# Layer 0 attention: products with values in groups of five steps instead of four, and two more buffers for exponentials

## The chip, the cores and the metric

The kernel runs on one core of a Trainium2 chip. The metric is the device time of one execution in microseconds (us); lower is better. Matrix products run on TensorE (PE in the profile, its weight loads PEld), elementwise work on VectorE (DVE) and GpSimd (POOL), activations such as the exponential on ScalarE (ACT). SyncE (SP) issues most of the DMA transfers.

## The reference, cut to what matters

Two layers over 2048 latent tokens and 256 context tokens. The even layer (layer 0) runs two branches side by side: latent attention with 8 heads over all 2304 keys, and a gated linear attention ("GLA"), scanned in both directions. The odd layer has a neighbourhood attention. The change is inside the latent attention of layer 0:

```python
s = jnp.einsum('bqhd,bkhd->bhqk', qi, k, preferred_element_type=jnp.float32) * scale
p = jax.nn.softmax(s, axis=-1).astype(v.dtype)
return jnp.einsum('bhqk,bkhd->bqhd', p, v)
```

Scores have 96 components per head, values 64. Context queries see the 256 context keys only; latent queries see all 2304.

## The kernel before, in words

The program is written with a tile framework. It records instructions in the order of the Python code, and a scheduler then puts each engine's instructions into one fixed order, by the program's order, by when it expects data and buffers to be ready, and by explicit "issue after" edges. At run time every engine works through its own list in order and waits on semaphores. So a change in one loop can move instructions of another branch that share its engines.

**Attention of layer 0** (`even_attention`, L867). The 8 heads are taken as 4 pairs, `j` = 0 to 3. Each pair has five query blocks, `nb` = 0 to 4: one of 256 context tokens (two key tiles) and four of 512 latent tokens (18 key tiles each). One key tile of one block is a **step**; a pair has 2 + 4 x 18 = 74 steps, the whole attention 296. A step does, for each of the two heads `i`:

- three matmuls into one of three PSUM buffers `st` (L980 to L982): high part of keys by high part of queries, high by low, low by high. Keys are the stationary operand, so scores come out transposed, keys on partitions;
- one exponential on ACT into a buffer `apt` of 128x512 (L984, shown at L106, the line of the helper);
- one addition on DVE into `acc`, the running sum of exponentials (L971).

The products with values come later. Each step is put on a list `pend` (L989). When `pend` holds six steps, the oldest four go through `tail` (L916): for each step and head one product (L922) of values (64 columns, stationary) with the exponentials, accumulated in PSUM `av`. Head 0 fills rows 0 to 63 of the PSUM tile, head 1 rows 64 to 127. In the trace every such product is two records of MATMUL, so a group of four steps, 8 products, shows as `x16`. Two steps after the last tail of a block, `end` (L927) runs `finish` (L849): a product `den` (L854) for the row sums, a reciprocal through Ln and Exp on ACT, three DVE operations (L859 to L861), one multiplication on POOL (L863) and the store.

**Loads.** `queries` (L907) loads one block of queries into one of two buffers `aq`: 96 rows of four parts (L910) and one further row (L911), both issued by SP. A block's load can start when the scores of the block two before it are done. At a new pair, the block of 512 queries after the context block therefore waits for the last scores of the previous pair, and so does the last third of the keys' low part (`akl`, L892), which SP issues ahead of it. The context block in between has two steps only. Values come as `av<-Vn` (L899) in thirds.

**What else runs.** The GLA (`gla`, L686) shares all engines. Per chunk of 128 tokens PE runs L722 and L728 (gates), L739 and L743 (cumulative sums), L766 (transposes), L776 (scores inside the chunk), L785 and L791 (products with values), with ACT and DVE steps between them. After the last chunk DVE walks the backward scan (L814 to L816: three operations for each of 16 chunks); only when it is done does the output loop go on (L830: product with the scanned state, L842: transposes), because its output tile takes a buffer of the scan. `even_mix` (L1009) also splits the output weights in this time (`wraw<-w_out`, L380 and L383), and after the attention it runs the projection.

Of the kernel before, what the change touches and what calls it, by code (L numbers as in the profile page):

```python
# [17 lines left out]
P = 128  # L18
# [70 lines left out]
class Kern:  # L89
# [777 lines left out]
    def even_attention(self, ap, pp):  # L867
        nc = self.nc
        blocks = [(0, CTX, [0, 1])] + [(CTX + 512 * b, 512, list(range(NT))) for b in range(4)]
        TT = NT // 3  # L870
        W = TT * P
        ring = [self.tl(ap, [P, 2, W], f"akh{n}", F32R, bufs=1) for n in range(4)]
        self.att_free = ring[0]
        for kh in ring:
            nc.gpsimd.memset(kh[A_QK : A_QK + 1].bitcast(F32), 1.0)
        K, L, V = {}, {}, {}

        def parts(j, p):
            return ((0, W // 2), (W // 2, W)) if j + p == 0 else ((0, W),)

        def keys(j, p):

            K[j, p] = kh = ring[(3 * j + p) % 4]
            for a, b in parts(j, p):
                nc.sync.dma_start(kh[:A_QK, :, a:b].bitcast(F32),
                                  self.KT[2 * j : 2 * j + 2, 0, :A_QK, p * W + a : p * W + b].rearrange("h p t -> p h t"))
                yield

        def low(j, p):
            L[j, p] = kl = self.tl(ap, [P, 2, W], "akl", F32R, bufs=3)  # L890
            for a, b in parts(j, p):
                nc.sync.dma_start(kl[:A_QK, :, a:b].bitcast(F32),  # L892
                                  self.KT[2 * j : 2 * j + 2, 1, :A_QK, p * W + a : p * W + b].rearrange("h p t -> p h t"))
                yield

        def values(j, p):
            V[j, p] = v = self.tl(ap, [P, TT, P], "av", bufs=4)
            for a, b in parts(j, p):
                nc.sync.dma_start(v[:, a // P : b // P, :], self.Vn[:, (p * W + a) // P : (p * W + b) // P, j * P : j * P + P])  # L899
                yield  # L900

        def load(*gens):
            for g in gens:
                for _ in g:
                    pass

        def queries(j, q0, w):  # L907

            q = self.tl(ap, [P, 4, 512], "aq", F32R, bufs=2)
            nc.sync.dma_start(q[:A_QK, :, :w].bitcast(F32), self.QT[2 * j : 2 * j + 2, :, :A_QK, q0 : q0 + w].rearrange("h z p t -> p (h z) t"))  # L910
            return q, nc.sync.dma_start(q[A_QK : A_QK + 1, 0::2, :w].bitcast(F32),  # L911
                                        self.QT[2 * j : 2 * j + 2, 0, A_QK : A_QK + 1, q0 : q0 + w].rearrange("h p t -> p h t"))

        pend, late, O = [], [], {}

        def tail(j, nb, n, kt, pts):  # L916

            w, kts = blocks[nb][1:]
            if n == 0:
                O[j, nb] = self.tl(pp, [P, 512], "av", bufs=2)  # L920
            for i in range(2):
                nc.tensor.matmul(O[j, nb][i * 64 : i * 64 + 64, :w], V[j, kt // TT][:, kt % TT, i * 64 : i * 64 + 64], pts[i][:, :w],  # L922
                                 start=n == 0, stop=n == len(kts) - 1)
            if n == len(kts) - 1:
                late.append([2 if nb else 5, j, nb])

        def end(j, nb):  # L927
            q0, w, _ = blocks[nb]
            zt = self.tl(ap, [P, 512], "azt", bufs=2)
            nc.sync.dma_start(zt[:, :w], self.zaT[j, :, q0 : q0 + w])  # L930
            self.finish(O.pop((j, nb))[:, :w], sums.pop((j, nb)), zt[:, :w], self.RT[j, :, q0 : q0 + w], w, ap, pp, ("den", 1))

        def step_late():
            for x in late:
                x[0] -= 1
                if x[0] <= 0:
                    end(*x[1:])
            late[:] = [x for x in late if x[0] > 0]

        early, sums, first = {}, {}, {}  # L940
        for j in range(4):
            if j == 0:
                early[0], _ = queries(0, 0, CTX)
                gens = [keys(0, 0), low(0, 0), values(0, 0)]
                for g in gens:
                    next(g)
                early[1], _ = queries(0, CTX, 512)
                for g in gens:
                    next(g)
                for p in (1, 2):  # L950
                    load(keys(0, p), low(0, p), values(0, p))
            else:
                load(low(j, 2), values(j, 1), values(j, 2))
            for nb, (q0, w, kts) in enumerate(blocks):
                if j == 0 and nb in early:
                    Q = early.pop(nb)
                else:
                    Q, last = queries(j, q0, w)
                if j < 3 and nb in (2, 3):
                    with self.tc.issue_after(last.ins):  # L960
                        load(keys(j + 1, 0) if nb == 2 else values(j + 1, 0))
                yield
                acc = [self.tl(ap, [P, 512], f"acc{i}") if nb else self.tl(ap, [P, CTX], f"accc{i}", bufs=1) for i in range(2)]

                def add(n, pts):
                    for i in range(2):
                        if n == 0:
                            first[i] = pts[i]
                        else:
                            a = first[i] if n == 1 else acc[i]  # L970
                            nc.vector.tensor_tensor(out=acc[i][:, :w], in0=a[:, :w], in1=pts[i][:, :w], op=ALU.add)  # L971

                for n, kt in enumerate(kts):
                    pts = []
                    kq = slice(kt % TT * P, kt % TT * P + P)
                    kh, kl = K[j, kt // TT], L[j, kt // TT]
                    for i in range(2):
                        qh, ql = Q[:, 2 * i, :], Q[:, 2 * i + 1, :]
                        ps = self.tl(pp, [P, 512], "st", bufs=3)
                        nc.tensor.matmul(ps[:, :w], kh[: A_QK + 1, i, kq], qh[: A_QK + 1, :w], start=True, stop=False)  # L980
                        nc.tensor.matmul(ps[:, :w], kh[:A_QK, i, kq], ql[:A_QK, :w], start=False, stop=False)  # L981
                        mm = nc.tensor.matmul(ps[:, :w], kl[:A_QK, i, kq], qh[:A_QK, :w], start=False, stop=True)  # L982
                        pt = self.tl(ap, [P, 512], "apt", bufs=14)
                        self.act(pt[:, :w], ps[:, :w], AF.Exp, scale=A_SCALE)  # L984
                        pts.append(pt)
                    add(n, pts)
                    if n == len(kts) - 1:
                        sums[j, nb] = [a[:, :w] for a in acc]
                    pend.append((j, nb, n, kt, pts))  # L989
                    with self.tc.issue_after(mm.ins):  # L990
                        step_late()
                        if len(pend) == 6:
                            for _ in range(4):
                                tail(*pend.pop(0))
                    if nb == 4 and j < 3 and n % TT == TT - 1 and n < NT - 1:
                        load(keys(j + 1, n // TT + 1), low(j + 1, n // TT))
        yield mm
        while pend:
            tail(*pend.pop(0))
        while late:  # L1000
            step_late()
# [759 lines left out]
```

## Time and profile before

| what | value |
|---|---|
| median of 3 runs | 3673.76 us (3667.17 to 3674.72) |
| the profiled execution | 3676.2 us |
| its span | 3674.1 us |
| mean granted clock of TensorE | 0.982 |
| attention of layer 0 on PE | from 1086.0 to about 1982 us of the span |

The span is the stretch of the profiled execution that the profiler covers; 2.1 us of that execution lie outside it. In the views, a row of the order of time gives start, duration, engine, line, operation, output and inputs, and in brackets how long the engine sat idle before it and who released it. Matmuls are pipelined: each record lasts longer than the distance to the next, so distances between starts are what PE spends.

### The profile page before, as it was taken

How to read it: one execution, taken by the hardware profiler on the slowest of the kernel's cores; microseconds unless marked ns; L12 is line 12 of the kernel's file. 1: busy time of each engine (PE TensorE's matmuls, PEld its weight loads, DVE VectorE, ACT ScalarE, POOL GpSimd, SP SyncE). 2: the span in 40 equal slices, each digit the busy share in tenths (PEclk: the TensorE clock that was granted, in tenths of full speed). 3: DMA queues.
4: the chain of work that ended last, by engine and by line, in shares of the span. 5: the costliest groups of instructions: out<-in, count | busy, mean ns of one | idle time of the engine just before them, and what ended most of it. 6: DMA issues, size and time to landing. Idle time of an engine off the chain costs nothing.

```text
span 3674.1 us, 51831 instructions
## 1 busy us (share of the span) xinstructions
PE 3565.7 (97%) x18404; PEld 2758.7 (75%) x18404; DVE 2363.0 (64%) x4860; ACT 1437.0 (39%) x2741; POOL 1205.6 (33%) x1336
## 2 busy tenths in 40 slices
PE   8999999999999999999999999999899999999998
PEld 6988998888886666655556878888688887555577
DVE  4677666888876666687664444454578784666721
ACT  5545551111125555555553124444422223555510
POOL 1433330101111212122201233333334443777743
PEclk9999999999999999999999999999999999999899
DMA  7455472222241232243622544455744447788554
GB/s 253 145 155 155 133 210 87 80 73 88 75 137 53 83 98 79 85 115 109 177 67 96 188 161 123 141 157 160 227 146 122 146 120 190 210 215 219 175 178 149
DMA packets 364372, 512.19 MB, mean 139 GB/s; under 512 B 25825, under 2 KB 243889, under 8 KB 358210
## 3 DMA queue, kind: packets, MB, share of 16 engines
q1 hardware_dynamic: 322642, 425.49, 39.8%
q0 software_dynamic: 19872, 55.92, 5.1%
q10 hardware_dynamic: 21600, 27.46, 2.1%
q8 instruction: 146, 2.39, 0.3%
q14 instruction: 112, 0.92, 0.1%
HBM read 329.38 MB, written 179.37 MB: 138 GB/s over the span
## 4 chain that ended last, share of the span: by engine, by line
PE 69%; issue 15%; POOL 5%; DVE 5%; DMA 4%; ACT 2%; SPq 0%; POOLq 0%; DVEq 0%; ACTq 0%
PE av L922 7%; PE gm L129 6%; PE gm L130 6%; PE gm L131 6%; PE st L980 4%; PE st L981 4%; PE st L982 4%; PE st L129 2%; PE st L131 2%; PE st L130 2%; PE pj L131 2%; PE pj L130 2%; PE pj L129 2%; PE o L1456 2%; DMA wraw<-w_od 1%
## 5 line engine op out<-in xcount | busy, mean ns | idle before, releaser
L971 DVE TENSOR_TENSOR acc<-acc,apt 128x512 f32<-128x512 f32 x512 | 364.8, 737 | 153.5 <-ACT apt L106 150.6
L106 ACT ACTIVATE apt<-st 128x512 f32<-128x512 f32 (+1 forms) x592 | 344.6, 594 | 290.5 <-PE st L982 257.4
L662 DVE TENSOR_REDUCE mm<-mx 128x1 f32<-128x512 f32 (+1 forms) x656 | 393.2, 630 | 89.9 <-PE mx L661 81.8
L922 PE MATMUL av<-apt,av 128*64 128x512 f32 (+1 forms) x1184 | 286.4, 599 | 0.0
L980 PE MATMUL st<-aq,akh 97*128 97x512 f32 (+1 forms) x592 | 255.7, 432 | 9.7 <-DMA aq<-QT 6.1
L661 PE MATMUL mx<-mk,mq 96*128 96x512 f32 (+1 forms) x656 | 238.6, 372 | 0.0
L981 PE MATMUL st<-aq,akh 96*128 96x512 f32 (+1 forms) x592 | 236.7, 400 | 0.0
L982 PE MATMUL st<-aq,akl 96*128 96x512 f32 (+1 forms) x592 | 235.3, 398 | 0.0
L1330 DVE CUSTOM_DVE_ANT_1 mx<-mx,mtab 128x217 f32<-128x217 f32 (+11 forms) x576 | 184.6, 338 | 49.2 <-PE mx L1324 37.9
L106 ACT ACTIVATE opt<-opt 128x930 f32<-128x930 f32 (+9 forms) x144 | 119.2, 830 | 248.0 <-POOL opt L1627 141.0
L106 ACT ACTIVATE u<-gm 128x352 f32<-128x352 f32 (+1 forms) x144 | 70.5, 496 | 360.4 <-PE gm L131 208.7
L1587 DVE TENSOR_TENSOR opt<-st,tab 128x64 f32<-128x64 f32 (+10 forms) x576 | 142.8, 316 | 88.2 <-PE st L1424 58.1
L922 PEld LDWEIGHTS av<-apt,av 128*64 128x64 f32 x1184 | 81.9, 138 | 156.4 <-issue 154.8
L980 PEld LDWEIGHTS st<-aq,akh 97*128 97x128 f32 x592 | 113.5, 192 | 101.6 <-issue 49.5
L1462 POOL TENSOR_TENSOR oacc<-oacc,opt 128x682 f32<-128x682 f32 (+10 forms) x144 | 169.8, 1199 | 26.4 <-ACT opt L106 25.1
L982 PEld LDWEIGHTS st<-aq,akl 96*128 96x128 f32 x592 | 114.6, 194 | 25.8
L661 PEld LDWEIGHTS mx<-mk,mq 96*128 96x128 f32 x656 | 122.7, 188 | 11.7
L981 PEld LDWEIGHTS st<-aq,akh 96*128 96x128 f32 x592 | 115.3, 195 | 18.3
L1423 PE MATMUL st<-q,kt 128*128 128x480 f32 (+5 forms) x256 | 99.6, 391 | 23.8 <-DVE opt L1587 18.9
L106 ACT ACTIVATE x<-px,modB,modA 128x128 f32<-128x128 f32 x272 | 99.3, 469 | 58.1 <-PE px L331 46.3
L129 PE MATMUL gm<-w0h,hhi 128*128 128x512 f32 x288 | 116.1, 403 | 0.0
L129 PE MATMUL gm<-w1h,hhi 128*128 128x512 f32 x288 | 115.7, 402 | 0.0
(570 smaller groups left out, 9928.1 us busy)
## 6 DMA issues: line engine op xcount, KB each, us to landing
q<-Q SPq DMA_DIRECT2D x48, 512.0 KB
H<-x ACTq DMA_DIRECT2D x36, 512.0 KB
adaw<-ada_w SPq DMA_DIRECT2D x64, 256.0 KB
x<-H SPq DMA_DIRECT2D x32, 512.0 KB
wraw<-w_od SPq DMA_DIRECT2D x64, 256.0 KB
K1t<-okt POOLq DMA_DIRECT2D x32, 512.0 KB, 7.6
kt<-K1t SPq DMA_DIRECT2D x32, 512.0 KB
mtab<-rpb_q SPq DMA_DIRECT2D x16, 899.0 KB
```

Source lines behind the costliest of these rows:

```text
L106: return self.nc.scalar.activation(out, in_, func, **kw)
L129: self.nc.tensor.matmul(out, lh(k), rh(k), start=j == 0, stop=False)
L130: self.nc.tensor.matmul(out, lh(k), rl(k), start=False, stop=False)
L131: yield self.nc.tensor.matmul(out, ll(k), rh(k), start=False, stop=j == n - 1)
L661: mm = nc.tensor.matmul(ps[:, :w], q[:A_QK, (t % 6) * P : (t % 6) * P + P], k[:A_QK, k0 : k0 + w], start=True, stop=True)
L662: nc.vector.tensor_reduce(out=m[:, t, n : n + 1], in_=ps[:, :w], axis=AX.X, op=ALU.max)
L922: nc.tensor.matmul(O[j, nb][i * 64 : i * 64 + 64, :w], V[j, kt // TT][:, kt % TT, i * 64 : i * 64 + 64], pts[i][:, :w], start=n == 0, stop ...
L971: nc.vector.tensor_tensor(out=acc[i][:, :w], in0=a[:, :w], in1=pts[i][:, :w], op=ALU.add)
L980: nc.tensor.matmul(ps[:, :w], kh[: A_QK + 1, i, kq], qh[: A_QK + 1, :w], start=True, stop=False)
L981: nc.tensor.matmul(ps[:, :w], kh[:A_QK, i, kq], ql[:A_QK, :w], start=False, stop=False)
L982: mm = nc.tensor.matmul(ps[:, :w], kl[:A_QK, i, kq], qh[:A_QK, :w], start=False, stop=True)
L1330: nc.vector.tensor_tensor_reduce(out=s, in0=s, in1=tb[:, ri : ri + rn, ci : ci + cn], scale=1.0, scalar=-3e38, op0=ALU.add, op1=ALU.max, a ...
```

## The change

The list of pending steps is allowed to grow to seven, and five steps then go through `tail` in one group. Two buffers are added for the exponentials, since two more of them are held. Nothing is computed differently: each of the 592 products (L922) is still there.

```diff
-                        pt = self.tl(ap, [P, 512], "apt", bufs=14)
+                        pt = self.tl(ap, [P, 512], "apt", bufs=16)
...
-                        if len(pend) == 6:
-                            for _ in range(4):
+                        if len(pend) == 7:
+                            for _ in range(5):
                                 tail(*pend.pop(0))
```

A full group is 10 products in place of 8. With six as the limit, groups go out at steps 6, 10, 14 and so on, counted over all pairs; with seven at steps 7, 12, 17 and so on.

## The prediction

> **What bounds the kernel now.** I read the page first, for the busy shares and the groups of the attention, then the busy time by stretch.
>
> ```profile
> span 3674.1 us, 51831 instructions
> PE 3565.7 (97%) x18404; PEld 2758.7 (75%) x18404; DVE 2363.0 (64%) x4860; ACT 1437.0 (39%) x2741; POOL 1205.6 (33%) x1336
> ...
> L971 DVE TENSOR_TENSOR acc<-acc,apt 128x512 f32<-128x512 f32 x512 | 364.8, 737 | 153.5 <-ACT apt L106 150.6
> ...
> L922 PE MATMUL av<-apt,av 128*64 128x512 f32 (+1 forms) x1184 | 286.4, 599 | 0.0
> ```
>
> ```profile
> core 0: us, PE busy (x) PEld busy (x) DVE busy (x) ACT busy (x) POOL busy (x), PEclk, DMA share, GB/s
> 1096.00:1585.00 489.00, 487.56 (x2520) 308.78 (x2519) 328.52 (x464) 269.42 (x540) 101.31 (x98) 1.00 0.30 87
> 1585.00:1675.00 90.00, 84.73 (x362) 49.42 (x361) 86.12 (x124) 43.72 (x79) 13.53 (x10) 0.96 0.27 76
> 1675.00:1982.00 307.00, 302.16 (x1364) 183.62 (x1365) 195.38 (x291) 167.50 (x332) 58.44 (x57) 0.97 0.38 107
> ```
>
> The attention has three stretches. In the first, 489 us, PE is busy 487.56 us and DVE two thirds: PE bounds it. In the second, 90 us, DVE walks the scan of the GLA and is busy 86.12 us: there DVE bounds, and PE time saved is not gained. In the third PE bounds again. So the change can gain only PE time in the first and third stretch, and can lose where PE waits.
>
> **What a group costs.** In the order of time on PE:
>
> ```profile
> 1704.83 0.40 PE L982 MATMUL st<-aq,akl 96*128 96x512 f32 x1
> 1705.15 3.65 PE L922 MATMUL av<-apt,av 128*64 128x512 f32 x16
> 1708.74 0.50 PE L980 MATMUL st<-aq,akh 97*128 97x512 f32 x1
> 1709.08 0.39 PE L981 MATMUL st<-aq,akh 96*128 96x512 f32 x1
> 1709.31 0.40 PE L982 MATMUL st<-aq,akl 96*128 96x512 f32 x1
> ...
> 1734.19 0.40 PE L982 MATMUL st<-aq,akl 96*128 96x512 f32 x1
> 1734.51 1.08 PE L854 MATMUL den<-acc,mtwos 128*64 128x512 f32 x4
> 1735.52 0.50 PE L980 MATMUL st<-aq,akh 97*128 97x512 f32 x1
> 1735.86 0.40 PE L981 MATMUL st<-aq,akh 96*128 96x512 f32 x1
> ```
>
> Score matmuls start 0.23 us apart (1709.08 to 1709.31). From the L982 ahead of a group to the L981 behind it 4.25 us pass; without a group it would be 0.46, so 8 products cost 3.79. A `den`, two products of the same shape, costs 1.67 less 0.46, 1.21. Eight products are four pairs, two are one: three pairs cost 2.58, one pair 0.86, and what is left, **0.35 us, is the fixed price of a run**. A larger group saves that price.
>
> A group that the scheduler cuts at an odd product loses more: seven products take 3.58 us, as eight do, and the eighth alone 1.00.
>
> ```profile
> 1311.89 3.65 PE L922 MATMUL av<-apt,av 128*64 128x512 f32 x14
> 1315.47 0.66 PE L766 MATMUL gl<-ident,gkt 128*128 128x128 f32 x4
> ...
> 1316.17 1.07 PE L922 MATMUL av<-apt,av 128*64 128x512 f32 x2
> 1317.17 0.39 PE L980 MATMUL st<-aq,akh 97*128 97x256 f32 x1
> ```
>
> I count in the instruction order of the built kernels. Before: 90 runs of L922 that take the time of 311 pairs (the 592 products are 296 pairs; cuts waste 15). After: 72 runs, 307 pairs. In PE time that is 18 x 0.35 + 4 x 0.86 = 9.7 us. Of it two runs and two pairs (2.4 us) lie in the scan stretch; a `den` (1.2 us) also leaves that stretch for the first. What counts is 9.7 - 2.4 - 1.2 = **6.1 us**. Five steps' worth of single scores (3.5 us) move from the third stretch into the first, which is neutral. In the scan stretch DVE's list between the second and last scan step is 117 operations in place of 121: three of 256 columns (0.43) and one of 512 (0.69) fewer, **2.0 us**.
>
> ```profile
> 1602.13 0.69 DVE L971 TENSOR_TENSOR acc<-acc,apt 128x512 f32<-128x512 f32 x1
> 1602.73 0.43 DVE L859 TENSOR_TENSOR den<-den,rc 128x256 f32<-128x256 f32 x1
> ```
>
> The two buffers keep the slack: at a group's start 14 tiles of 16 are held, where 12 of 14 were. They add no instruction, so I put them at zero. They shift the later tiles by 4 KB, and the projection's tiles then lie over other old ones; an estimate from the 0.69 us of one DVE operation bounds what a few later releases cost by 0 to 2 us. The stretch of the scan also ends in a wait of PE and a half clock of 10.24 us (rows further down); DVE's scan sets that moment before and after, and I leave it, with half of a 6.8 us step of the clock, 3.4 us, as its bound to either side.
>
> **What a group hid.** At a new pair of heads the block of 512 queries waits for a buffer that the last scores of the old pair free, and its load is issued only then, behind `akl`:
>
> ```profile
> 1558.08 0.40 PE L982 MATMUL st<-aq,akl 96*128 96x512 f32 x1
> 1560.08 3.65 PE L922 MATMUL av<-apt,av 128*64 128x512 f32 x16
> 1566.95 0.47 PE L980 MATMUL st<-aq,akh 97*128 97x512 f32 x1 [1.24 <-DMA aq<-QT]
> ...
> 1782.14 0.77 PE L980 MATMUL st<-aq,akh 97*128 97x512 f32 x1 [4.84 <-DMA aq<-QT]
> ```
>
> ```profile
> 1312.37 0.44 SPq L910 DMA_DIRECT2D aq<-QT  x1
> ```
>
> ```profile
> 1558.88 7.98 DMA aq<-QT
> ...
> 1771.16 10.89 DMA aq<-QT
> ```
>
> From issue to use the load takes 7.98 us at pair 2 and 10.89 at pair 3. At pair 1 it was issued at 1312.37 and its user started at 1320.49 without a wait: at most 8.1. Before, a group stood in each of the three gaps: groups go out at steps 74, 150 and 222, and pairs begin after 74, 148 and 222. After, they go out at 72 and 77, at 147 and 152, and at 222: **pairs 1 and 2 lose their cover of 3.6 us, pair 3 gets 0.86 us more.** In the new order the gap holds, besides 12 scores of the context block (0.12 each, 1.44), at pair 1 L791, L739, L743 and L766 twice four, at pair 2 L776, L728 and L785:
>
> ```profile
> 1569.29 0.87 PE gl L739 x4
> 1570.15 0.79 PE gl L743 x8
> ...
> 1574.36 0.88 PE gl L766 x8
> ...
> 1578.55 1.09 PE gl L776 x16
> ...
> 1583.81 0.89 PE gl L785 x8
> 1584.70 0.91 PE gl L791 x8
> ```
>
> With 0.4 for changes of shape (an estimate) that is 5.3 us at pair 1 and, with 0.24 for L728, 4.0 at pair 2, against a landing 8.4 us after the release (0.4 to the issue, 7.98). PE then idles 3.1 us at pair 1, none before, and 4.4 at pair 2, 1.2 before: **+3.1 and +3.2 us**. Bounds: the GLA's own waits can't make it more, since they lie inside; a load landing at 5.3 makes it 0 and -1; one of 10.9 adds 2.9 to each. Pair 3: **-0.9**. Behind the waiting L980 all of PE's list is queued, and ACT behind it.
>
> **The clock.** PE's granted clock falls behind such waits:
>
> ```profile
> 1564.95:1568.37 3.42, 2.18 (x13) 1.81 (x13) 1.39 (x2) 1.58 (x3) 1.72 (x1) 1.00 1.07 238
> ...
> 1595.67:1599.09 3.42, 1.87 (x9) 1.07 (x8) 3.29 (x5) 2.04 (x5) 2.17 (x2) 1.00 0.17 61
> 1599.09:1605.91 6.82, 6.82 (x18) 3.65 (x19) 6.70 (x11) 3.43 (x7) 1.61 (x1) 0.50 0.29 77
> ...
> 1674.18:1684.42 10.24, 9.62 (x27) 5.76 (x29) 5.96 (x10) 5.89 (x15) 2.92 (x3) 0.50 0.27 78
> ```
>
> A stretch of 3.42 us with 2.18 busy kept the full clock; one with 1.87 was followed by 6.82 us at half. So a wait above about 1.5 us in such a stretch costs half of 6.8, 3.4 us. Pair 2's wait should bring this in full, **+3.4**; pair 1's, split by GLA work, half of it, **+1.7** (bounds 0 and 5.1, half of the 10.24).
>
> [...]
>
> **The sum.** -6.1 - 2.0 + 3.1 + 3.2 - 0.9 + 3.4 + 1.7 = **+2.4 us**. Against the profiled execution (3676.2, its span 3674.1 and 2.1 outside) that is 3678.6; the median, 3673.76, lies 2.4 us lower and gives 3676.2. I say 3677, no measurable change: about 0.2%, 7.3 us, is what a measurement of this kernel can tell.
>
> **The rivals.**
>
> - *The loads land in time* (faster). If the query loads of pairs 1 and 2 land within 5.3 and 4.0 us of the release, no new wait arises and pair 2's old one goes: -6.1 - 2.0 - 0.9 - 1.2 = -10.2, 3664. For it: nothing shows when pair 1's load landed. Against: 7.98 and 10.89. Chance 0.10.
> - *The waits come, the clock stays.* Without 3.4 and 1.7 the sum is -2.7, 3671. For it: both waits are cut up by GLA work, and the stretch with 2.18 busy. Against: the one with 1.87. [...] Chance 0.17, nearly all within 0.2%.
> - *The loads land late* (slower). In the new order the last thirds of values (L899), freed by later tails, are issued just ahead of pair 2's queries, and a chunk of the GLA's input just behind pair 1's. If both loads then take pair 3's 10.89 us, each wait grows by 2.9 and pair 1's clock falls in full, +1.7: +2.4 + 5.8 + 1.7 = +9.9, 3684 on the median, 3686 on the profiled execution; it decides from about 9.6 us on (2.4 + 1.7 + twice 1.6 passes 7.3). For it: the same load took 7.98 and 10.89 by what ran beside it. Against: at pair 3 the load of a gate row (L1120) went out just before, which the other two gaps don't have. Chance 0.20.
> - *Longer groups starve DVE in the scan stretch.* A group lasts 0.9 us longer, without new exponentials; if DVE runs dry six times, +5.2, and 3682. Against: DVE was busy 86.12 of 90 us there across groups of 3.6. Chance 0.08.
> - That the scheduler undoes the grouping is settled by the built order: 44 of 72 runs have all ten products.
>
> The forecast keeps 0.45. **Range**: from 3664 (loads in time) to 3689 (late loads, 3686, and the scan stretch's bound of 3.4). **Chances**: faster 0.17 (0.10 and the forecast's lower edge), slower 0.28 (0.20, half of the starving, and the upper edge), same 0.55.
>
> **What would show it.** In the profile after: L922 as `x20` in the third stretch, 4.65 us in all (five pairs of 0.86 and 0.35); no group between the last scores of pairs 0 and 1 and the next pair's first block of 512; L980 there with idle time ended by `aq<-QT`, of about 3 and 4 us, and a half clock behind; pair 3's wait down to about 4. Wrong it would be if those waits are absent or above 6 us, if the clock falls elsewhere in the first stretch, or if the scan stretch lengthens.

## The result, and the profile after

The changed kernel took 3681.78 us (median; 3675.30 to 3687.67) beside 3673.03 us of the kernel before: ratio 1.0029, 95% interval 1.0022 to 1.0037. Measured once more: 3679.88 beside 3671.46 us, 1.0019 (1.0009 to 1.0030). So it is slower by some 8.6 us, a quarter of a per cent. The forecast was +2.4 us and "no measurable change"; the time lies inside its range, on the slow side, but both intervals leave out 1: the change can be measured, and that was not forecast.

The page of the changed kernel (group rows: count, busy us, mean ns of one, then the idle time before them):

```profile
span 3679.9 us, 51810 instructions
...
L922 PE MATMUL av<-apt,av 128*64 128x512 f32 (+1 forms) x1184 | 276.5, 594 | 0.0
L980 PE MATMUL st<-aq,akh 97*128 97x512 f32 (+1 forms) x592 | 254.4, 430 | 12.7 <-DMA aq<-QT 10.2
```

The same 1184 records of L922 take 9.9 us less than before (286.4); in the mean of three profiles of either order of PE, 285.4 and 276.9, it is 8.5. The change does what it says. The second row holds the other side: PE's idle time ahead of L980, most of it ended by the query load.

Busy time by stretch, cut near the same events as in the prediction's table (the columns are the same):

```profile
core 0: us, PE busy (x) PEld busy (x) DVE busy (x) ACT busy (x) POOL busy (x), PEclk, DMA share, GB/s
1096.00:1599.00 503.00, 494.99 (x2558) 317.28 (x2558) 333.19 (x474) 272.93 (x549) 101.82 (x100) 0.99 0.30 85
1599.00:1683.00 84.00, 76.64 (x337) 45.67 (x337) 81.46 (x117) 41.57 (x75) 11.48 (x9) 0.98 0.27 74
1683.00:1985.00 302.00, 294.73 (x1346) 180.16 (x1346) 205.10 (x288) 164.17 (x327) 61.76 (x57) 0.98 0.39 108
```

The first stretch is 14 us longer (489 before), the scan stretch 6 shorter (90), the third 5 shorter (307). Cut exactly at the first and third group of L830, the three differences are +12.6, -3.9 and -5.1. The first stretch also holds more work: 2558 matmul records for 2520. In the first, 1.44 us of 489 were idle on PE; now 8.01 of 503 are.

The three gaps at new pairs, in the order of time on PE (start, duration, instruction; in brackets the idle time before it and what ended it). At pair 1 no group of L922 stands between the last scores of the old pair and the first block of 512:

```profile
1308.49 0.40 PE L982 MATMUL st<-aq,akl 96*128 96x512 f32 x1
...
1311.92 0.95 PE L743 MATMUL gl<-ind,gG 128*128 128x2 f32 x8
1313.52 0.63 PE L766 MATMUL gl<-ident,gqt 128*128 128x128 f32 x4 [0.65 <-DVE gqt L753]
1314.97 1.09 PE L766 MATMUL gl<-ident,gkt 128*128 128x128 f32 x4 [0.82 <-DVE gkt L753]
1317.29 0.77 PE L980 MATMUL st<-aq,akh 97*128 97x512 f32 x1 [1.24 <-DMA aq<-QT]
...
1318.28 0.63 PE L982 MATMUL st<-aq,akl 96*128 96x512 f32 x1
1318.71 0.63 PE L980 MATMUL st<-aq,akh 97*128 97x512 f32 x1
```

PE idles 0.65 + 0.82 + 1.24 = 2.71 us, where it did not idle before. The first two pieces name the GLA, but they lie within the time in which the load is on its way. Behind the wait scores start 0.43 us apart (1318.28 to 1318.71) and not 0.23: the half clock, granted from 1314.87 on (rows below). Pairs 2 and 3:

```profile
1558.54 0.40 PE L982 MATMUL st<-aq,akl 96*128 96x512 f32 x1
...
1562.88 1.13 PE L785 MATMUL gl<-gu,gat 128*128 128x128 f32 x8 [0.99 <-PE gl L728]
1567.07 0.47 PE L980 MATMUL st<-aq,akh 97*128 97x512 f32 x1 [3.07 <-DMA aq<-QT]
...
1767.73 4.51 PE L922 MATMUL av<-apt,av 128*64 128x512 f32 x20
...
1781.11 0.77 PE L980 MATMUL st<-aq,akh 97*128 97x512 f32 x1 [5.90 <-DMA aq<-QT]
```

4.06 us of idle time at pair 2 (1.24 before). At pair 3 the group is there, `x20`, and yet PE idles 5.90 us, more than the 4.84 of before. The loads behind these waits, from the chains of waits of the three gaps (start, us):

```profile
1309.29 7.90 DMA aq<-QT
...
1559.35 7.63 DMA aq<-QT
...
1769.28 11.69 DMA aq<-QT
```

Each gap brings a stretch at half clock (granted clock 0.50): from 1314.87, 1567.45 and 1779.08 on, at pairs 1 and 3 before the wait is over, which ends at 1317.29 and 1781.11. The rows of 3.41 us ahead of them are at full clock (stretch, its length, PE busy; PEclk and DMA share are the third and second numbers from the end):

```profile
1311.46:1314.87 3.41, 2.04 (x18) 1.74 (x16) 2.84 (x3) 2.45 (x8) 3.24 (x3) 1.00 1.06 247
1314.87:1321.70 6.83, 5.50 (x14) 3.07 (x16) 1.47 (x2) 1.79 (x3) 1.38 (x3) 0.50 1.06 254
1564.04:1567.45 3.41, 0.38 (x2) 0.36 (x3) 0.57 (x1) 0.60 (x1) 0.00 (x0) 1.00 1.07 248
1567.45:1570.86 3.41, 3.41 (x10) 2.65 (x9) 0.00 (x0) 1.19 (x2) 0.00 (x0) 0.50 1.06 252
1775.67:1779.08 3.41, 0.00 (x0) 0.00 (x0) 1.44 (x3) 0.57 (x2) 1.20 (x2) 1.00 1.15 218
1779.08:1785.91 6.83, 4.80 (x11) 3.80 (x12) 0.00 (x0) 1.72 (x3) 0.00 (x0) 0.50 0.96 268
```

The load isn't late by itself, the 16 DMA engines are busy while it is under way: their share is 0.96 to 1.15 in these rows, at 218 to 268 GB/s.

### The profile page after: what moved, and what is told of

Its sections match the earlier page's. It is cut to its first block, busy times and chain, and to the rows that moved or that the text cites. A ratio compares the mean times of both kernels' runs of the same rounds, so it can differ in the third digit from the quotient of the medians.

```text
span 3679.9 us, 51810 instructions
## 1 busy us (share of the span) xinstructions
PE 3561.2 (97%) x18404; PEld 2761.6 (75%) x18404; DVE 2373.2 (64%) x4860; ACT 1436.8 (39%) x2741; POOL 1208.2 (33%) x1336
## 4 chain that ended last, share of the span: by engine, by line
PE 68%; issue 14%; DVE 6%; DMA 5%; POOL 3%; ACT 3%; SPq 0%; POOLq 0%; DVEq 0%; ACTq 0%
PE av L922 7%; PE gm L129 6%; PE gm L130 6%; PE gm L131 6%; PE st L980 4%; PE st L981 3%; PE st L982 3%; PE o L1456 2%; PE st L129 2%; PE st L131 2%; PE st L130 2%; PE st L1423 2%; PE pj L129 2%; PE pj L131 2%; PE pj L130 2%
## 5 line engine op out<-in xcount | busy, mean ns | idle before, releaser
L971 DVE TENSOR_TENSOR acc<-acc,apt 128x512 f32<-128x512 f32 x512 | 378.0, 766 | 126.3 <-ACT apt L106 123.6
L922 PE MATMUL av<-apt,av 128*64 128x512 f32 (+1 forms) x1184 | 276.5, 594 | 0.0
L980 PE MATMUL st<-aq,akh 97*128 97x512 f32 (+1 forms) x592 | 254.4, 430 | 12.7 <-DMA aq<-QT 10.2
L982 PE MATMUL st<-aq,akl 96*128 96x512 f32 (+1 forms) x592 | 236.0, 399 | 0.0
L1330 DVE CUSTOM_DVE_ANT_1 mx<-mx,mtab 128x217 f32<-128x217 f32 (+10 forms) x576 | 184.3, 338 | 46.4 <-PE mx L1324 37.8
L922 PEld LDWEIGHTS av<-apt,av 128*64 128x64 f32 x1184 | 81.9, 137 | 157.1 <-issue 154.9
L980 PEld LDWEIGHTS st<-aq,akh 97*128 97x128 f32 x592 | 113.8, 192 | 85.8 <-issue 44.1
L982 PEld LDWEIGHTS st<-aq,akl 96*128 96x128 f32 x592 | 114.7, 194 | 25.6
L981 PEld LDWEIGHTS st<-aq,akh 96*128 96x128 f32 x592 | 115.3, 195 | 18.8
```

Source lines behind the costliest of these rows:

```text
L1330: nc.vector.tensor_tensor_reduce(out=s, in0=s, in1=tb[:, ri : ri + rn, ci : ci + cn], scale=1.0, scalar=-3e38, op0=ALU.add, op1=ALU.max, a ...
```

## The experiments

**Theory A**: in the gaps of pairs 1 to 3, PE waits for the query load, because groups of five go out beside the gaps and not in them, and behind each wait the half clock doubles the loss. **Theory B**: the two buffers, by shifting later tiles, delay the work behind the attention. **Theory D**: the loss lies elsewhere. C, that the load's time doesn't depend on what is ahead of it in the queue, is the rival on the repair; in the expectations of the first four runs C still stands for the prediction's rival that longer groups starve DVE. Where an expectation names a wait of an earlier profile, its figure can be up to 1.0 us above the idle time of the rows.

All ratios are against the kernel before. "Attention" runs from the start of the first score to that of the last L922. "Half clock" is the sum of such stretches inside it, without the one of 3.4 to 10.2 us that in 11 of the 14 profiles begins within 2.1 us of the first score. "Behind" is the rest of the span. All three come from one profile each, of a run that can lie 10 us off its median (that of `e4_shift` took 3683.50).

| kernel | median us, ratio (95%) | attention | half clock | behind |
|---|---|---|---|---|
| before; its second profile | see above | 885.7; 887.1 | 23.9; 20.5 | 1702.4; 1698.1 |
| changed; measured again | 1.0029 (1.0022 to 1.0037); 1.0019 (1.0009 to 1.0030) | 889.4; 892.7 | 23.9; 27.3 | 1705.4; 1705.9 |
| e1_buffers | 3672.65, 1.0002 (0.9994 to 1.0011) | 882.9 | 17.1 | 1699.6 |
| e2_five14 | 3681.76, 1.0027 (1.0017 to 1.0036) | 891.0 | 30.7 | 1701.4 |
| e3_cover | 3666.61, 0.9982 (0.9973 to 0.9991) | 879.2 | 10.2 | 1699.4 |
| e4_shift | 3673.86, 1.0008 (0.9998 to 1.0017) | 886.0 | 17.1 | 1707.7 |
| e5_aqfirst4 | 3668.19, 0.9986 (0.9975 to 0.9996) | 882.3 | 23.9 | 1697.4 |
| e6_aqfirst5 | 3671.40, 0.9993 (0.9985 to 1.0002) | 879.1 | 20.5 | 1703.8 |
| e7_both | 3663.10, 0.9972 (0.9961 to 0.9984) | 871.6 | 6.8 | 1702.2 |
| e8_values | 3678.10, 1.0015 (1.0005 to 1.0024) | 887.2 | 23.9 | 1704.5 |
| e9_akl | 3671.48, 1.0000 (0.9991 to 1.0009) | 875.5 | 17.1 | 1703.5 |
| e10_fill | 3679.94, 1.0019 (1.0010 to 1.0029) | 891.7 | 23.9 | 1701.4 |

### The two parts of the change, each alone

`e1_buffers`: the kernel before with 16 buffers.

```diff
-                        pt = self.tl(ap, [P, 512], "apt", bufs=14)
+                        pt = self.tl(ap, [P, 512], "apt", bufs=16)
```

> Groups of four as before, sixteen buffers for the exponentials: the second half of the change alone. Theory A (uncovered query loads): no group moves, so the time of before within 0.1%, about 3673 us, and no wait at pairs 1 and 2 beyond the 1.2 us of before. Theory B (the shift of later tiles by 4 KB costs something in the projection and the odd layer): slower than before by 3 to 8 us, all of it behind 1972 us of the span. Theory C (longer groups starve DVE and ACT): 3673 us, as A.

`e2_five14`: the changed kernel with 14 buffers.

```diff
-                        pt = self.tl(ap, [P, 512], "apt", bufs=16)
+                        pt = self.tl(ap, [P, 512], "apt", bufs=14)
```

> Groups of five with the fourteen buffers of before: the first half of the change alone. Theory A: the waits at pairs 1 and 2 stay as in the changed kernel (3.5 and 4.5 us), the time too, 3680 to 3682 us; at a full list every buffer is held, which may add 1 to 3 us where ACT waits for a buffer. Theory B: the later tiles lie as before, so 3674 to 3677 us. Theory C: as the changed kernel or slower.

The buffers alone change nothing (1.0002), and the groups alone lose the whole (1.0027). Theory B falls; the buffers are worth zero, as the prediction had it.

### The cover alone, and its loss without groups of five

`e3_cover`: the changed kernel, with a first group of two steps, so that groups of five go out at steps 74, 149 and 224 and again cover all three gaps.

```diff
-        pend, late, O = [], [], {}
+        pend, late, O, size = [], [], {}, [4]
...
-                        if len(pend) == 7:
-                            for _ in range(5):
+                        if len(pend) == size[0]:
+                            size[0] = 7
+                            while len(pend) > 2:
```

> The changed kernel with a first group of two steps once four are pending, then groups of five: groups go out at steps 74, 149 and 224 and stand again in all three gaps between pairs. Theory A: waits at pair 1 gone, at pair 2 under 1.5 us, at pair 3 at most 6; the clock no longer falls at pairs 1 and 2; 8 to 11 us less than the changed kernel, 3671 to 3674 us, so as before or a little faster. Theory B: 3680 us still, the loss being behind the attention. Theory C: 3680 us still.

3666.6 us: about 15 less than the changed kernel and 6 less than before. Pair 2's gap, in the order of time on PE:

```profile
1555.29 0.40 PE L982 MATMUL st<-aq,akl 96*128 96x512 f32 x1
...
1556.32 4.51 PE L922 MATMUL av<-apt,av 128*64 128x512 f32 x18
...
1561.18 1.07 PE L922 MATMUL av<-apt,av 128*64 128x512 f32 x2
1563.89 0.40 PE L980 MATMUL st<-aq,akh 97*128 97x512 f32 x1
```

The first score of the new block comes 8.6 us after the last of the old pair, as late as without a group (8.53), but without idle time and without a half clock behind it (the scores there start 0.23 to 0.24 us apart). What the load needs is the same; the group fills it. At pair 3 a wait of 4.14 us remains, and at pair 1 one of 1.77, which theory A had gone: there SP issued the last third of values (L899, 1312.75) between `akl` (1311.73) and the query load (1313.17), and the first score came 11.2 us after the last of the old pair (8.8 in the changed kernel, 8.9 in the one before). Of the 16.4 us between the spans of the changed kernel and of this one, 10.2 lie in the attention and 6.0 behind it, where the order of PE's instructions in the odd layer is again that of before; so not all of the gain is the cover's.

`e4_shift`: groups of four as before, shifted by a first group of three steps, so that they go out at 73, 77, 149, 221 and 225 and leave gaps 1 and 3 uncovered.

```diff
-        pend, late, O = [], [], {}
+        pend, late, O, size = [], [], {}, [5]
...
-                        if len(pend) == 6:
-                            for _ in range(4):
+                        if len(pend) == size[0]:
+                            size[0] = 6
+                            while len(pend) > 2:
```

> Groups of four and fourteen buffers as before, but with a first group of three steps, so that groups go out at steps 73, 77, 149, 221 and 225: pairs 1 and 3 lose their cover, pair 2 keeps it. Theory A: a new wait of 2 to 4 us at pair 1 with a half clock behind it, the wait at pair 3 up from 4.8 to about 8 us, pair 2 as before; 6 to 9 us slower than before, 3679 to 3682 us. Theory B and C: the size of the groups and the buffers are those of before, so 3673 us.

The waits came where theory A put them (pairs 1 and 3, none at pair 2):

```profile
1320.74 0.47 PE L980 MATMUL st<-aq,akh 97*128 97x512 f32 x1 [3.44 <-DMA aq<-QT]
...
1779.01 0.77 PE L980 MATMUL st<-aq,akh 97*128 97x512 f32 x1 [7.94 <-DMA aq<-QT]
```

The time did not follow: 1.0008, as theories B and C had it. PE idles 18.8 us in its attention, 11.7 to 13.7 in three profiles with the order of before, but in its order the scheduler cuts fewer groups at odd places. Its L922 runs number 84 and take the time of 303 pairs (90 and 311 before): at the prediction's prices 6 x 0.35 + 8 x 0.86 = 9.0 us less, about what was expected as the loss; the records of L922 are busy 278.8 us, 6.6 less than the mean of before. That this paid for the waits is argued and not shown. So the run shows the waits and not their price: that a shift changes where groups are cut was left out of its expectation.

### What is ahead of the query load

`e5_aqfirst4` (the kernel before) and `e6_aqfirst5` (the changed kernel) both issue `akl` and the later thirds of values behind the first 512-query load of a new pair. Their scores stand two lines lower, at L982 to L984.

```diff
-                load(low(j, 2), values(j, 1), values(j, 2))
+                pass
...
                     Q, last = queries(j, q0, w)
+                    if j and nb == 1:
+                        load(low(j, 2), values(j, 1), values(j, 2))
```

> Groups of four as before; only the load order at a new pair changes: the last third of the keys' low part (akl, 96 x 2 x 768 values, 590 KB) and the two later thirds of values are issued behind the first 512-query load of the pair and not ahead of it. Theory A (PE waits at new pairs for this query load, and the 590 KB ahead of it in the queue are a good part of its 8 to 11 us): the load lands about 3 us earlier, the wait of 1.5 us at pair 2 goes, that of 5.1 us at pair 3 shrinks to about 2, and half a step of half clock goes with them: 3 to 8 us less than before, 3665 to 3670. Theory C (the load's time is its own latency or the traffic of the other queues, not what is ahead of it): the waits stay and the time is that of before, ratio 1.000.

> Groups of five, 16 buffers, and the query load of a new pair ahead of akl as in the run with groups of four. Theory A (what the change loses, it loses in waits for this load at pairs 1, 2 and 3: about 3.7, 4.7 and 6.2 us in its profile, and in the half clock behind them): each shrinks by about 3 us and most of the half clock goes, 8 to 13 us less than the changed kernel, 3668 to 3674, at or below the kernel before. Theory D (the loss lies elsewhere, in the scan stretch or behind the attention): the time stays within 3 us of the changed kernel's 3682.

The times came as theory A had them: 3668.2 and 3671.4, the latter 8.5 us below the changed kernel of the same measurement. The same edit gains 3.3 us in the kernel before and 8.5 in the changed one, so 5.2 of the 8.4 us between these two hang on this load. The half clock did not go: 23.9 and 20.5 us are left. The two loads of the changed order, from the chains of waits of `e6_aqfirst5`, took 7.90 and 7.63 us before the edit:

```profile
1311.57 5.96 DMA aq<-QT
...
1556.91 5.52 DMA aq<-QT
```

About 2 us less, some 2.4 us earlier counted from the release, since the issue of `akl` is no longer ahead: an estimate from the 590 KB and the 248 to 254 GB/s of the rows at pairs 1 and 2 is 2.3 to 2.4 us. Theory C falls.

`e9_akl` moves `akl` alone, `e8_values` the values alone.

```diff
-                load(low(j, 2), values(j, 1), values(j, 2))
+                load(values(j, 1), values(j, 2))
...
+                    if j and nb == 1:
+                        load(low(j, 2))
```

> The changed kernel with akl alone behind the first 512-query load of a new pair; the values stay ahead. Theory A (the 590 KB of akl ahead of the query load make the waits): nearly all of the 8.5 us that both loads together gained, 3671 to 3674; from the last scores of the old pair to the first of the new block about 6.5, 6 and 10 us in place of 9.2, 9.0 and 13.6. Rival (the values made half of it): 3676 to 3678.

3671.5: moving `akl` alone in the program gives the whole repair. From the last score of the old pair to the first of the new block 6.2, 6.5 and 7.6 us pass, where the changed kernel had 8.8, 8.5 and 13.7. The third figure, expected at 10, is not `akl`'s alone: in the built order the last third of values went behind the query load of pair 3 as well (L910 at 1761.55, L899 at 1763.66).

```diff
-                load(low(j, 2), values(j, 1), values(j, 2))
+                load(low(j, 2))
...
+                    if j and nb == 1:
+                        load(values(j, 1), values(j, 2))
```

> The changed kernel with the loads of the two later thirds of values behind the first 512-query load of a new pair; akl stays ahead of it. In the built order this swaps one pair of instructions only: at pair 3 the last third of values (L899), which the changed kernel issues between the two parts of the query load, goes behind both. Theory A (pair 3's wait grew from 5.1 to 6.1 us because of that transfer, though the gap holds 0.86 us more work): the first scores of pair 3 come 1.5 to 2 us earlier after the last of pair 2 (13.6 before the edit, 11.8 in the kernel before the change), the wait is 4 to 4.5 us, and the time 1 to 2 us less than the changed kernel, 3679 to 3681. Rival (the third of values has no part in it; the loads of the output loop around it do it): the wait stays at 6 us and the time at 3680 to 3682.

This one swaps a single pair of SP's instructions. SP's list at pair 3 of the changed kernel (L910 and L911 are the two parts of the query load):

```profile
1767.83 0.32 SPq L892 DMA_DIRECT2D akl<-KT  x1
1768.20 0.44 SPq L910 DMA_DIRECT2D aq<-QT  x1
1768.85 0.38 SPq L899 DMA_DIRECT2D av<-Vn  x1
1769.28 0.57 SPq L911 DMA_DIRECT2D aq<-QT  x1
```

and of `e8_values`, with PE's first scores behind the wait, from the order of time of SP and of PE:

```profile
1772.87 0.44 SPq L910 DMA_DIRECT2D aq<-QT  x1
1773.36 0.57 SPq L911 DMA_DIRECT2D aq<-QT  x1
1774.03 0.73 SPq L899 DMA_DIRECT2D av<-Vn  x1
...
1782.29 0.47 PE L982 MATMUL st<-aq,akh 97*128 97x512 f32 x1 [2.42 <-DMA aq<-QT]
```

With the third of values out of the way the wait at pair 3 falls from 5.90 to 2.42 us, more than expected (4 to 4.5). The loads of the output loop go out behind it as before, the first (L827) 2.2 us after the query load in both profiles. So the longer wait of the changed kernel there is that transfer's. The median, 1.0015, can't be told from that of the changed kernel by its interval; the row can.

### Keeping PE busy in the gap

`e10_fill` adds 12 products to each gap of the changed kernel: work that the reference doesn't have and nobody reads.

```diff
+                if j and nb == 1:
+                    ps = self.tl(pp, [P, 512], "st", bufs=3)
+                    for n in range(12):
+                        nc.tensor.matmul(ps[:, :], K[j, 0][: A_QK + 1, 0, :P], K[j, 0][: A_QK + 1, 1, :512], start=n == 0, stop=n == 11)
```

> The changed kernel with 12 more products of 512 columns (0.23 us each, 2.8 us; of the first third of keys with itself, into a score buffer that nobody reads) between the context block and the first 512 block of pairs 1, 2 and 3. They do nothing but keep PE busy while the query load is on its way. Theory A (behind a wait PE runs at half clock for 6.8 us, and that costs as much as the wait): the waits fall under about 3 us with 1.9 busy and more in each stretch of 3.4 us, the half clock behind pairs 1 and 2 goes, that behind pair 3 perhaps; 5 to 9 us less than the changed kernel, 3671 to 3675, though no work is saved. Rival (the half clock is not set by the waits, or costs nothing because DVE or ACT bound there): the time stays at 3680 to 3683; if the added products push the first scores back, 1 to 3 us more.

A miss: 3679.94, as the changed kernel and as the rival had it. The added 2.8 us stand in the gaps and the time doesn't grow by them, but the half clock stayed, 23.9 us of it. The stretches of 3.41 us ahead of its falls at pairs 1 and 2:

```profile
1314.06:1317.47 3.41, 2.30 (x15) 1.89 (x15) 0.47 (x2) 1.25 (x5) 0.20 (x1) 1.00 1.05 294
1563.23:1566.64 3.41, 1.55 (x11) 1.24 (x9) 0.64 (x1) 0.60 (x1) 0.00 (x0) 1.00 1.05 246
```

Even with 2.30 us busy the clock fell. What the half clock alone costs, apart from the wait, is therefore not shown by a run; it stands on the 0.43 us from score to score. That half of theory A, the clock behind the waits doubling the loss, is not shown.

### The changed kernel and the kernel before again, and the best version

> The changed kernel once more, on the same chip as the repaired load order, for a second profile: its attention took 889.4 us, 3.6 more than before, its median 9 more. Theory A: the waits at pairs 1 and 2 are there again, with 3 to 5 us each, and the part behind the attention (1705.4 us against 1702.4) goes either way; the half clock in the attention sums to 12 to 24 us in steps of 3.41, where the first profile had 20.5 behind waits. Theory D: the part behind the attention is 3 us longer again, and the attention only 3 to 4 us.

The same waits (1.68 us ended by the load at pair 1, 3.50 at pair 2, 5.77 at pair 3), and again a longer part behind the attention.

> The kernel before once more, for a second profile. Theory A (the loss sits in the attention; what is left of the difference is half clock that falls differently from run to run): the attention takes 882 to 886 us again, against 889 to 893 in the three profiles with groups of five, with PE waiting 1.2 us at pair 2 and 5 us at pair 3 and none at pair 1. Theory D (the part behind the attention is longer with groups of five): it takes 1702 us or less here, where the three had 1705.4, 1705.9 and 1701.4.

885.7, 887.1 and, in `e1_buffers` with the same order, 882.9 us of attention against 889.4, 892.7 and 891.0 with groups of five: 885.2 and 891.0 in the mean, **5.8 us**. Behind the attention 1700.0 against 1704.2, **4.2 us**. Theory A holds for the first as far as the waits go, and theory D has a part of its own in the second, though single profiles of one order scatter by over 4 us there (1698.1 to 1702.4). Where it lies, by the rows of L922 and L1317 (maxima of the odd layer) in the kernel before and, behind it, in the changed one (first and last start stand ahead of the last column):

```profile
L922 PE MATMUL av<-apt,av x1184: 379/592/1116, 1096.6 to 1971.7; 128*64 128x512 f32 x192, 128*64 128x256 f32 x6
...
L1317 PE MATMUL mx<-mk,mz x256: 275/281/365, 2646.9 to 3049.9; 128*128 128x256 f32 x128
```

```profile
L922 PE MATMUL av<-apt,av x1184: 378/593/1117, 1097.1 to 1974.5; 128*64 128x512 f32 x192, 128*64 128x256 f32 x6
...
L1317 PE MATMUL mx<-mk,mz x256: 275/281/366, 2652.9 to 3055.3; 128*128 128x256 f32 x128
```

From the last L922 to the last L1317 1078.2 us pass before and 1080.8 after; in the second profiles 1076.5 and 1081.3. The built order explains that something can differ so far from the change: the scheduler, whose expected times have shifted, places some 20 of PE's instructions of the odd layer elsewhere in every kernel with groups of five but `e3_cover` (the first L1317 comes 13 records later), and some of ACT and DVE in the projection. One part can be placed. Counted in PE's matmul records from the last L922 on, the 3041st to the 3300th are the same products in every kernel. They take 53.0 us in the six profiles in which PE has the old order there (`e3_cover`, `e4_shift` and `e5_aqfirst4` among them) and 54.8 in the eight with the new one, PE idling 0.78 and 0.47 us for DVE in it. So 1.8 of the 4.2 us go with the new order of PE. The rest stays open: `e4_shift` has the old order there and still takes 1080.7 us to its last L1317.

`e7_both` joins the two repairs, `e3_cover` and the query load ahead.

> Both repairs: a first group of two steps and then groups of five, which puts a group into every gap at a new pair, and the query load ahead of akl. Theory A: the waits at pairs 1 and 2 are gone already with the cover (3666.6), the one left, 4.4 us at pair 3, shrinks to about 1.5 and loses its half clock: 3 to 6 us less, 3661 to 3664. Theory C: 3666 to 3667, as with the cover alone.

3663.1 us, ratio 0.9972 (0.9961 to 0.9984): faster than both kernels, by 8.4 us and, against the changed kernel as measured again with it, 16.8. The waits at pairs 1 and 2 are gone, and of half clock 6.8 us is left. At pair 3, 3.52 us of idle time remain, twice the expected: though first in the queue, the load took 9.7 us there, with `akl` and the load of the next block issued within 2 us behind it.

## Why the prediction was right or wrong

- **What a group costs: right.** 72 runs that take the time of 307 pairs, as counted; L922 is busy 9.9 us less, and 8.5 in the mean of three profiles, where the working has 9.7.
- **The scan stretch: right in kind, more than forecast.** Between the first and the third group of L830 83.4 us pass in place of 87.3 in all three profiles of either order: -3.9, the forecast -2.0. DVE takes 80.2 us in place of 82.8 from the second to the last step of the scan, with four operations fewer, as counted; the other 1.3 us are not explained. Longer groups did not starve DVE, so that rival is out.
- **New waits at pairs 1 and 2: right.** 2.71 and 4.06 us of idle time for the forecast 3.1 and 4.4; the loads landed 7.9 and 7.6 us after their issue, not at the late-loads rival's 10.89. `e3_cover` shows at pair 2 that the lost cover is the cause. The gaps held 6.1 and 4.5 us of work, for 5.3 and 4.0 in the working, whose 0.4 for changes of shape has no row behind it.
- **Half clock behind them: there, but its price in the sum is wrong.** Behind pair 1 it lasted 6.83, 6.83 and 10.24 us in three profiles, behind pair 2 3.41, 6.83 and 6.83. At 0.20 of every 0.43 us lost, that is at most 4.8 to 7.9 us together, for the forecast 5.1. But the step added it to the half clock of before as it stood. The kernel before has a fall of 3.41 to 6.83 us behind pair 2 or early in the scan stretch that then stays away, and PE waits through part of the new stretches (5.50 us busy of 6.83 behind pair 1, 4.80 of 6.83 at pair 3). Half of PE's busy time at half clock is 13.9, 12.0 and 10.5 us in the attention before and 12.3, 14.8 and 11.3 with groups of five: +0.7 in the mean, less than the scatter.
- **Pair 3: wrong.** The step "Pair 3: -0.9" took the landing of before and only added work to the gap. The load landed 1.9 us later (release to first score 13.7, 11.8 before), because the last third of values went out in the middle of it: PE idled 5.90 us for 4.84, +1.1 and not -0.9 (5.6 for 4.7 in the mean of three profiles). The rival of late loads named this very transfer, L899, and put it at pair 2, where it went out six microseconds ahead and did no harm. `e8_values` takes it away.
- **The sum: wrong beyond the gaps.** The same terms, each as the mean of three profiles of either order less that of the other (us; "matmul time" is PE's busy time in the attention, with half clock counted half):

| term | forecast | measured |
|---|---|---|
| matmul time | -9.7 | -6.2 |
| idle time in the three gaps | 3.1 + 3.2 - 0.9 = +5.4 | +7.0 |
| idle time elsewhere in the attention | 2.4 + 1.2 - 2.0 = +1.6 | +4.3 |
| half clock | +5.1 | +0.7 |
| attention | +2.4 | +5.8 |
| behind the attention | 0 | +4.2 |

So the loss is idle time. That the forecast for the attention is only 3.4 us off is in part errors of opposite sign: matmul time fell 3.5 us less, PE idled 1.6 us more in the gaps and 2.7 elsewhere, and the half clock gave 4.4 of it back. Of the idle time outside the gaps some 3 us are waits of L842, in the GLA's output loop, for POOL; in the profile of the kernel before, whose longest sums of waits follow, there is none (us, times, longest):

```profile
PE st L980 <- DMA aq<-QT: 6.1, 2, 4.8
PE gl L830 <- ACT gsb L106: 3.7, 1, 3.7
```

and in that of the changed kernel:

```profile
PE st L980 <- DMA aq<-QT: 10.2, 3, 5.9
PE gl L830 <- ACT gsb L106: 4.8, 1, 4.8
PE gl L842 <- POOL goi L839: 3.4, 3, 1.3
```

What brought these waits was not tried. I had read the order on each engine around the change, and not to its end. That the time lies in the range is partly luck: its upper end was set by the rival of late loads, whose late loads at pairs 1 and 2 did not come.

- **The rival that the clock stays: ruled out.** The clock fell behind stretches of 3.41 us with 2.04 and, in `e10_fill`, 2.30 us of PE busy: 1.37 and 1.11 us of idle time in them, less than the 1.5 us of the step "The clock".

## What to carry to other kernels

Ahead of an engine that is 97% busy, ask of each block of work which latency it happens to cover: here a group of products stood in each gap behind a buffer's release, and a change that saved some 8.5 us of L922 moved it out. Ask also what stands in the queue ahead of a load that can start only at a release: here 590 KB that are first needed 12 steps later put it back by 2.3 and 2.5 us at pairs 1 and 2 of the changed kernel (beside `e6_aqfirst5`), and by 2.1 and 2.4 us at pairs 2 and 3 of the kernel before (beside `e5_aqfirst4`). Being first is not all: at pair 3 of `e7_both` the load still took 9.7 us. And where a scheduler works with expected times, compare the order to the end of the program, not only around the change.

## What the runs showed of the hardware

Behind the first scores, the half clock of the attention began at 1314.87, 1567.45, 1680.10 and 1779.08 us in the profile of the changed kernel: 74, 33 and 29 times 3.41 us apart. In that of the kernel before it began at 1599.09, 1674.18 and 1780.00, 22 and 31 times 3.41 us apart. It lasted 3.41, 6.83 or 10.24 us, differing between profiles of one kernel (6.83, 6.83 and 10.24 behind pair 1 with groups of five). Counted over 14 profiles, of 44 such steps of 3.41 us at full clock in the attention with under 1.95 us of PE busy 42 were followed by half clock, between 1.95 and 2.5 us 5 of 29, above that none of 3437. In the two profiles named here it was 6 of 6, 1 of 6 and none of 492. That one, the step from 1311.46 at pair 1 of the changed kernel, has 2.04 us busy, and its idle time is in two pieces, 0.65 and 0.72 us.
